# Queries and values of the sparse attention split at their projections, the last gates tied to the memory branch, gate stores issued by ACT

## The chip, the cores and the metric

The kernel runs on one core of a Trainium2 chip. Five engines work side by side, each with its own queue of instructions that it takes in order: PE (TensorE, matrix products and transposes), DVE (VectorE), ACT (ScalarE), POOL (GpSimd) and SP (SyncE, which only issues DMA transfers here). The metric is the time of one execution on the device, in microseconds (us); lower is better.

## The reference

One inference step of a hybrid streaming encoder on 1024 prompt tokens and 64 sample tokens (1088 together, width 1024). What matters here:

```python
qa = rope(rmsnorm(qa.reshape(B, T, N_HEADS_A, HD_A), g_qa), pos)      # 8 heads of 64
ka = rope(rmsnorm(ka.reshape(B, T, N_KV_A, HD_A), g_ka), pos)         # 2 heads of 64
va = va.reshape(B, T, N_KV_A, HD_A)
...
logits = jnp.einsum('bthgd,btjhd->bthgj', q, k_sel, ...) * (HD_A ** -0.5)   # selected keys only
probs = jax.nn.softmax(logits, axis=-1).astype(va.dtype)
out = jnp.einsum('bthgj,btjhd->bthgd', probs, v_sel)
...
# memory branch: 4 heads of 128 against 256 memory tokens
logits = jnp.einsum('bthd,bmhd->bhtm', qm, mk, ...) * (HD_M ** -0.5)
return jnp.einsum('bhtm,bmhd->bthd', probs, mv).reshape(B, T, D_MEM_ATT)
...
ga, gb, gm = jnp.split(jax.nn.sigmoid(gates...), N_BRANCH, axis=-1)
mixed = ga * (a @ w_oa) + gb * (b @ w_ob) + gm * (m @ w_om)
```

After that come an output projection and a SwiGLU feed-forward, which the change does not touch.

## The kernel before

Precise products are made from split numbers: a float is kept as a rounded high part and a remainder (names with `hi`/`h` and `lo`/`l`), and one product becomes three matmuls, hi x hi, hi x lo and lo x hi. ACT or POOL makes the high part, DVE subtracts to get the low one. Tokens are worked on in nine blocks (eight of 128, one of 64).

The stages around the change, with their places in the profiled execution (us from the span's start):

- Queries of the memory branch are projected (326 to 397; `qn` stored to `q_m` in DRAM).
- Queries of the sparse attention, `w_qa`, in two halves of nine blocks (397 to 460). Each block is 24 matmuls from token blocks and a weight `tmhi`/`tmlo`, held in one buffer; then come four squares on ACT (`hjunk`), a power on POOL (`hr`), the scaling on DVE (`qn`), the rotation on DVE (`rope`, `qr`), and a store to `q_a` in DRAM. The selection of keys runs beside this on DVE and ACT.
- Keys and values, `w_kv` (460 to 530). A block's keys go through the same chain with two heads, then are split (`kd`: a cast on ACT, a subtraction on DVE), transposed four times on PE, copied by ACT (`kt`) and stored to `k_t`; values go to `v_a`.
- The memory branch (530 to 655), in steps `t` of two halves: queries are loaded (`qn<-q_m`), transposed and split (`qh`, `ql`); logits `lg`; softmax `ex`; probabilities are transposed and multiplied with the values.
- Attention (684 to 870), with blocks in the order 2, 0, 1, 3, 8, 4, 5, 6, 7. `queries_t` loads a block's queries, splits them (`qs`: cast on ACT, subtraction on DVE), transposes the eight heads on PE and copies the result on ACT into `qT`. Ahead of it all values are loaded (`vf`) and split into `vb` in ten pieces.

The order on each engine is fixed when the program is built, by a scheduler with priorities. Three groups of products have low priority and are scheduled where PE has nothing else (`fl` in PSUM, three banks): the gates (`fill_gate`; 96 products of 24 matmuls with `hh`, `hl`, a tanh on ACT into `fsg` and a store), the w_ob products (`fill_ob`, which load a gate as `fpt`), and the w_om products (`fill_om`, which load `gt`). The last 24 gates (72 to 95) go to `side_a`; before, the call for them stands behind the memory branch. SP issues all their stores, as nearly all other transfers. `raw`, `fraw` are loads of weights; a lane is one of eight semaphores that transfers take in turn, and an instruction that uses a transfer's result, or its lane again, waits for it.

Of the kernel before, what the change touches and what calls it, by code (L numbers as in the profile page):

```python
# [22 lines left out]
NB = 9  # L23
# [22 lines left out]
def encoder_step(ctx: ExitStack, tc: tile.TileContext, a: dict, o: list):  # L46
# [30 lines left out]
    def mm(dt=F32):  # L77
        return psum[0].tile([128, 512], dt, name="mm", tag="mm", bufs=n_mm[0])
# [22 lines left out]
    def wblock(src, shape, raw=None, hl_=None):  # L101
# [10 lines left out]
        lo_of(lo, raw, hi)  # L112
        return hi.rearrange(pat, **kw), lo.rearrange(pat, **kw)

    def matmul3(ps, pairs):
        n = len(pairs) * 3
        i = 0
        for lh, ll, rh, rl in pairs:
            for l, r in ((lh, rh), (lh, rl), (ll, rh)):
                PE.matmul(ps, l, r, start=i == 0, stop=i == n - 1)  # L120
                i += 1

    def rstd(r, ss, inv):
# [60 lines left out]
    side_m = dram.tile([KT, 2, 128, T], F32, name="side_m")  # L184
    side_a = dram.tile([KT, 2, 128, T], F32, name="side_a")
    gate_b = dram.tile([KT, 128, T], F32, name="gate_b")
    q_a = dram.tile([T, 512], F32, name="q_a")
    q_m = dram.tile([T, 512], F32, name="q_m")
    k_t = dram.tile([128, 2, 2, SEQ + PAST + DEC], F32, name="k_t")
    v_a = dram.tile([T, 128], F32, name="v_a")  # L190
    mem_k = dram.tile([256, 512], F32, name="mem_k")
    mem_v = dram.tile([256, 512], F32, name="mem_v")

# [3 lines left out]
    def raw_tile():  # L197
        return wp.tile([128, 1024], F32, name="raw", tag="raw", bufs=3)
# [274 lines left out]
    with tc.tile_pool(name="qa", bufs=1) as qp:  # L473
        cosa = qp.tile([128, NB, HDA], F32, name="cosa")
        sina = qp.tile([128, NB, HDA], F32, name="sina")

        def tables(gname, scale=None):
            SP.dma_start(cosa, a["cos_a"].rearrange("(b p) d -> p b d", p=128))
            SP.dma_start(sina, a["sin_a"].rearrange("(b p) d -> p b d", p=128))
            g1 = qp.tile([128, HDA], F32, name="g1", tag="g1", bufs=2)  # L480
            g2 = qp.tile([128, HDA], F32, name="g2", tag="g2", bufs=2)
            bcast_row(g1, a[gname], 0, HDA)
            bcast_row(g2[:, :32], a[gname], 32, 32)
            bcast_row(g2[:, 32:], a[gname], 0, 32)
            if scale:
                for g_ in (g1, g2):
                    G.tensor_scalar(g_, g_, scale, 1.0, op0=OP.mult, op1=OP.mult)
            G.tensor_tensor(cosa, cosa, g1[:, None, :].to_broadcast([128, NB, HDA]), op=OP.mult)
            G.tensor_tensor(sina, sina, g2[:, None, :].to_broadcast([128, NB, HDA]), op=OP.mult)

        tables("g_qa", -HDA ** -0.5)
        for half in range(2):
            w = tm_weights(qp, a["w_qa"][half], 256)
            for b in range(NB):
                t0, n = TS[b]
                ps = token_major(w, b, 256)
                qn = qp.tile([128, 4, HDA], F32, name="qn", tag="qn", bufs=2)
                head_norm(qp, ps, n, 4, HDA, qn[:n])
                qr = qp.tile([128, 4, HDA], F32, name="qr", tag="qr", bufs=2)
                rope(qp, qr[:n], qn[:n], n, 4, HDA, cosa[:, b], sina[:, b])  # L500
                SP.dma_start(q_a[t0:t0 + n, half * 256:(half + 1) * 256], qr[:n].rearrange("p h d -> p (h d)"))

        def key_split(src, n):
            kd = qp.tile([128, 2, 2, 2, HDA], F32R, name="kd", tag="kd", bufs=2)
            bc = src[:, :, None, :].to_broadcast([n, 2, 2, HDA])
            A.copy(kd[:n, :, 0], bc)
            V.tensor_tensor(kd[:n, :, 1], bc, kd[:n, :, 0].bitcast(F32), op=OP.subtract)
            return kd

        def keys_t(kd, n, c0):  # L510
            ps = mm(F32R)
            for j in range(4):
                PE.transpose(ps[:, j * 128:j * 128 + n],
                             kd[:n, j // 2, j % 2].rearrange("p s d -> p (s d)"), ident_r[:n, :n])
            kt = qp.tile([128, 2, 2, 128], F32R, name="kt", tag="kt", bufs=2)
            A.copy(kt[:, :, :, :n].rearrange("p k s t -> p (k s) t"), ps.rearrange("p (j t) -> p j t", j=4)[:, :, :n])
            SP.dma_start(k_t[:, :, :, c0:c0 + n], kt[:, :, :, :n].bitcast(F32))

        kc = raw_tile()[:, :128]
        SP.dma_start(kc, a["cache_a_k"])  # L520
        last = (key_split(kc.rearrange("p (k d) -> p k d", k=2), 128), 128, SEQ)
        tables("g_ka")
        w = tm_weights(qp, a["w_kv"], 256)
        for b in range(NB):
            t0, n = TS[b]
            ps = token_major(w, b, 256)
            kn = qp.tile([128, 4, HDA], F32, name="qn", tag="qn", bufs=2)[:, :2]
            head_norm(qp, ps[:, :128], n, 2, HDA, kn[:n])
            kr = qp.tile([128, 4, HDA], F32, name="qr", tag="qr", bufs=2)
            rope(qp, kr[:n, :2], kn[:n], n, 2, HDA, cosa[:, b], sina[:, b])  # L530
            A.copy(kr[:n, 2:].rearrange("p h d -> p (h d)"), ps[:, 128:])
            kf = kr[:n, :2].rearrange("p h d -> p (h d)")
            vf = kr[:n, 2:].rearrange("p h d -> p (h d)")
            SP.dma_start(o[2][t0:t0 + n] if b < 8 else o[8], kf)
            SP.dma_start(o[3][t0:t0 + n] if b < 8 else o[9], vf)
            SP.dma_start(v_a[t0:t0 + n], vf)
            kd = key_split(kr[:n, :2], n)
            if last:
                keys_t(*last)
            last = (kd, n, t0 if b < 8 else SEQ + PAST)  # L540
        keys_t(*last)
# [39 lines left out]

    for c0, cn in CH:
        for f, w in enumerate(first):
            SP.dma_start(gate_b[f, :, c0:c0 + cn], fsig(w, c0, cn))
    fill_gate(8, gate_b, 2, 8)
    fill_gate(16, side_m[:, 0], 0, 8)
    fill_ob()
# [2 lines left out]
    if True:  # L592
# [3 lines left out]
        with tc.tile_pool(name="matw", bufs=1) as mp:  # L596
# [33 lines left out]
            def queries(t0, n, half):  # L630
# [3 lines left out]
                for h in range(2):  # L634
                    PE.transpose(ps[:, h * n:(h + 1) * n], qn[:, h * 128:(h + 1) * 128], ident[:n, :n])
                return ps[:, :2 * n]

            for half in range(2):
                hs2 = slice(2 * half, 2 * half + 2)
# [80 lines left out]
                for t in range(11):  # L720
# [4 lines left out]
                    if 0 <= t - 3 < 8:  # L725
                        values_of(t - 3, exs[t - 3], pp_)
                    sample(t)


    rest = [(f, ci) for ci in range(3) for f in range(KT)]  # L730
    fill_gate(0, side_a[:, 0], 0, 8)
    for _ in range(1):
        fill_om(*rest.pop(0))
    kv_c = tc.tile_pool(name="kvp", bufs=1)
# [116 lines left out]

    aoh, aol = bh, bl
    ORDER = (0, 2, 1, 3)
    KEYS_AT = {0: (384, 768), 3: (768, SEQ + PAST + DEC)}
    with tc.tile_pool(name="att", bufs=1, side="right") as ap_:

        def wide(name):
            return ap_.tile([128, 1024], F32, name=name, tag="pr", bufs=11)

        vf = [wide("vf").rearrange("p (b c) -> p b c", c=128) for _ in range(2)]  # L860
        SP.dma_start(vf[0], v_a[:SEQ].rearrange("(b p) c -> p b c", p=128))
        SP.dma_start(vf[1][:, 0], a["cache_a_v"])
        SP.dma_start(vf[1][:64, 1], v_a[SEQ:])
        for b0, b1, n in ((0, 3, 128), (3, 6, 128), (6, 8, 128), (8, 9, 128), (9, 10, 64)):
            for kv in range(2):
                vs = vf[b0 // 8][:n, b0 % 8:b0 % 8 + b1 - b0, kv * HDA:(kv + 1) * HDA]
                A.copy(vb[:n, b0:b1, kv, 0], vs)
                lo_of(vb[:n, b0:b1, kv, 1], vs, vb[:n, b0:b1, kv, 0])

        def queries_t(b):  # L870
            t0, n = TS[b]
            q = ap_.tile([128, HA, HDA], F32, name="q", tag="q", bufs=2)
            ld = SP.dma_start(q[:n].rearrange("p h d -> p (h d)"), q_a[t0:t0 + n])
            if b in KEYS_AT:
                with tc.issue_after(ld.ins):
                    load_keys(*KEYS_AT[b])
            qs = ap_.tile([128, HA, 2, HDA], F32R, name="qs", tag="qs", bufs=1)
            A.copy(qs[:n, :, 0], q[:n])
# [588 lines left out]
```

## Time and profile before

| | |
|---|---|
| Median of 3 runs | 1745.0 us (1744.95 to 1747.08) |
| The profiled execution | 1742.28 us |
| Its span, first to last instruction | 1740.5 us |
| Mean granted clock of TensorE | 0.997 of full speed |
| PE, DVE, ACT, POOL busy | 97%, 68%, 46%, 24% of the span |

Busy shares are means over stages with different limits, so a stage has to be read by its own windows. A wait is put down to the engine whose semaphore came last. The span is what the trace shows; 1.8 us of the execution lie around it.

### The profile page before, as it was taken

Reading aid. Unit: us, or ns where it says so; the run is one execution under the profiler, and the core shown is the slowest. Engines: PE = TensorE matmul, PEld = TensorE weight load, DVE = VectorE, ACT = ScalarE, POOL = GpSimd, SP = SyncE. Lnnn points to the kernel's source line nnn. Section 1 sums busy time; section 2 is a strip of 40 time slices with the busy share of each in tenths; the row PEclk is TensorE's granted clock in tenths of the full one; section 3 lists DMA queues with packets and bytes.
Section 4 is the critical chain, followed back from the end, with each engine's and each line's share of the span. In section 5 each row is a group of like instructions: output and inputs, shape, how many; then the busy total and the mean of one; then the engine's idle time right before and its main releaser. Section 6 shows DMA issues by size and latency. Waiting matters only on the chain.

```text
span 1740.5 us, 32481 instructions
## 1 busy us (share of the span) xinstructions
PE 1687.7 (97%) x12074; PEld 1637.3 (94%) x12074; DVE 1181.5 (68%) x2597; ACT 809.0 (46%) x1949; POOL 409.6 (24%) x444
## 2 busy tenths in 40 slices
PE   7999999999999999899899999999999999999999
PEld 6999999999999999787698998999999999999999
DVE  6566999999964442788874687666658556465553
ACT  5457667746633441569722343334334333353431
POOL 4110423345511212775303442000101000000000
PEclk9999999999999999999999999999999999999999
DMA  7212541223367324760273326443545443497661
GB/s 233 65 62 67 173 138 47 71 84 109 95 183 223 106 93 144 260 196 2 87 259 114 118 82 220 167 142 106 191 145 179 148 153 121 136 349 256 207 195 53
DMA packets 154829, 251.38 MB, mean 144 GB/s; under 512 B 25127, under 2 KB 101279, under 8 KB 154670
## 3 DMA queue, kind: packets, MB, share of 16 engines
q1 hardware_dynamic: 154670, 249.30, 44.0%
q8 instruction: 95, 1.56, 0.4%
q14 instruction: 64, 0.52, 0.1%
HBM read 174.15 MB, written 75.09 MB: 143 GB/s over the span
## 4 chain that ended last, share of the span: by engine, by line
PE 59%; DVE 6%; DMA 4%; issue 2%; POOL 2%; ACT 2%; SPq 0%; DVEq 0%; ACTq 0%; POOLq 0%
PE mm L1129 24%; PE mm L1352 12%; PE mm L120 10%; PE fl L120 8%; PE acc L933 1%; PE tr L903 1%; DVE lo L86 1%; PE mm L926 1%; DVE wlo L86 1%; DVE fr L1083 1%; DMA u<-tg 1%; DMA side_a<-gt 1%; DMA gt<-side_m 0%; DVE ws L1090 0%; PE mm L615 0%
## 5 line engine op out<-in xcount | busy, mean ns | idle before, releaser
L1129 PE MATMUL mm<-hi,whi 128*128 128x288 f32 (+1 forms) x1120 | 323.0, 289 | 2.3 <-ACT whi L1121 2.3
L1129 PE MATMUL mm<-lo,whi 128*128 128x288 f32 (+1 forms) x1120 | 323.4, 289 | 0.0
L1129 PE MATMUL mm<-hi,wlo 128*128 128x288 f32 (+1 forms) x1120 | 323.4, 290 | 0.0
L1129 PEld LDWEIGHTS mm<-hi,whi 128*128 128x128 f32 x1120 | 211.8, 189 | 3.0 <-ACT whi L1121 3.0
L1129 PEld LDWEIGHTS mm<-lo,whi 128*128 128x128 f32 x1120 | 211.8, 189 | 0.0
L1129 PEld LDWEIGHTS mm<-hi,wlo 128*128 128x128 f32 x1120 | 211.0, 189 | 0.2 <-DVE wlo L86 0.2
L120 PE MATMUL fl<-hh,whi 128*128 128x362 f32 (+1 forms) x576 | 190.1, 331 | 0.4 <-ACT hh L133 0.4
L120 PE MATMUL fl<-hl,whi 128*128 128x362 f32 (+1 forms) x576 | 190.2, 330 | 0.0
L120 PE MATMUL fl<-hh,wlo 128*128 128x362 f32 (+1 forms) x576 | 189.8, 330 | 0.0
L1352 PE MATMUL mm<-uh,wh 128*128 128x256 f32 (+1 forms) x600 | 171.4, 289 | 0.9 <-ACT wh L1342 0.9
L1352 PE MATMUL mm<-ul,wh 128*128 128x256 f32 (+1 forms) x600 | 171.7, 288 | 0.0
L1352 PE MATMUL mm<-uh,wl 128*128 128x256 f32 (+1 forms) x600 | 170.4, 288 | 0.0
L120 PE MATMUL mm<-tmlo,hh 128*128 128x256 f32 (+3 forms) x432 | 123.0, 287 | 1.1 <-DVE tmlo L86 1.0
L120 PE MATMUL mm<-tmhi,hh 128*128 128x256 f32 (+3 forms) x432 | 121.8, 287 | 2.0 <-POOL tmhi L96 2.0
L120 PE MATMUL mm<-tmhi,hl 128*128 128x256 f32 (+3 forms) x432 | 122.5, 286 | 0.0
L86 DVE TENSOR_TENSOR wlo<-raw,whi 128x1024 fp32r<-128x1024 f32 (+1 forms) x75 | 75.2, 1014 | 65.2 <-ACT whi L1121 38.9
L777 ACT ACTIVATE junk_a<-score,cand_a,sgn_a 128x512 f16<-128x512 f32 (+2 forms) x93 | 95.5, 1027 | 41.9 <-DVE cand_a L794 21.8
L1352 PEld LDWEIGHTS mm<-uh,wh 128*128 128x128 f32 x600 | 112.4, 188 | 1.3 <-ACT wh L1342 1.3
L1352 PEld LDWEIGHTS mm<-ul,wh 128*128 128x128 f32 x600 | 112.7, 188 | 0.0
L1352 PEld LDWEIGHTS mm<-uh,wl 128*128 128x128 f32 x600 | 112.2, 188 | 0.1
L120 PEld LDWEIGHTS fl<-hh,whi 128*128 128x128 f32 x576 | 108.6, 189 | 1.4 <-issue 0.8
L120 PEld LDWEIGHTS fl<-hl,whi 128*128 128x128 f32 x576 | 108.5, 188 | 0.6
(395 smaller groups left out, 4563.0 us busy)
## 6 DMA issues: line engine op xcount, KB each, us to landing
uf<-u SPq DMA_DIRECT2D x75, 272.0 KB, 4.3
raw<-in_w_up_dram SPq DMA_DIRECT2D x26, 512.0 KB, 4.3
fraw<-in_w_gates_dram SPq DMA_DIRECT2D x24, 512.0 KB, 3.6
fr<-in_w_gate_dram SPq DMA_DIRECT2D x22, 512.0 KB, 4.2
dr<-in_w_down_dram SPq DMA_DIRECT2D x22, 512.0 KB, 5.7
s<-dr SPq DMA_DIRECT2D x22, 512.0 KB, 3.1
raw<-s SPq DMA_DIRECT2D x44, 256.0 KB, 3.8
side<-side_a SPq DMA_DIRECT2D x8, 1088.0 KB, 6.9
```

The costliest lines, as they stand in the source:

```text
L86: V.tensor_tensor(lo, src, hi.bitcast(F32), op=OP.subtract)
L120: PE.matmul(ps, l, r, start=i == 0, stop=i == n - 1)
L777: A.activation(junk[:n, :nk], sc, AF.Sign, bias=bj, scale=1.0 if scale is None else scale[:n, j:j + 1], accum_out=sj)
L903: PE.matmul(lg[:n, i * 512:i * 512 + cn], qT[:, h, :n], kT[:, kv, s, k0 + c:k0 + c + cn], start=s == 0, stop=s == 1)
L926: PE.transpose(pt[:cn, i * n:(i + 1) * n], probs[i][:, c:c + cn], ident[:n, :n])
L933: PE.matmul(acc, vv, r, start=ji == 0 and i == 0, stop=ji == nj - 1 and i == 1)
L1083: V.scalar_tensor_tensor(hb[e][:, :n], ys[i][:, kk], gffn_c[:, kk:kk + 1], rb[:, :n], op0=OP.mult, op1=OP.mult)
L1129: PE.matmul(dst[i], l, r, start=start and j == 0, stop=stop and j == 11, skip_group_check=True)
L1352: PE.matmul(acc[f, i], l[:, fs], r[:, cs], start=start and j == 0, stop=stop and j == 2, skip_group_check=True)
```

## The change

Queries are split and transposed where they are projected, and kept in DRAM transposed (`q_t`); attention loads `qT` with one transfer. Values are split where they are projected (`v_t`), and attention loads `vb` in two to three transfers, tied behind loads of queries. The last 24 gates are issued from inside the memory branch's steps, each tied behind a matmul of an earlier step. All gate stores are issued by ACT in place of SP. The tile pool `pr` of attention has 12 buffers for 11.

```diff
-    q_a = dram.tile([T, 512], F32, name="q_a")
+    q_t = dram.tile([NB, 128, HA, 128], F32, name="q_t")
-    v_a = dram.tile([T, 128], F32, name="v_a")
+    v_t = dram.tile([SEQ + PAST + DEC, 2, 2, HDA], F32, name="v_t")
...
+        def split(name, src, n, heads):
+            s = qp.tile([128, heads, 2, HDA], F32R, name=name, tag=name, bufs=2)
+            A.copy(s[:n, :, 0], src)
+            V.tensor_tensor(s[:n, :, 1], src, s[:n, :, 0].bitcast(F32), op=OP.subtract)
+            return s
+
+        def four_t(s, n, dst):
+            ps = mm(F32R)
+            for j in range(4):
+                PE.transpose(ps[:, j * 128:j * 128 + n], s[:n, j], ident_r[:n, :n])
+            t = qp.tile([128, 4, 128], F32R, name="kt", tag="kt", bufs=2)
+            A.copy(t[:, :, :n], ps.rearrange("p (j t) -> p j t", j=4)[:, :, :n])
+            SP.dma_start(dst, t[:, :, :n].bitcast(F32))
...
-                SP.dma_start(q_a[t0:t0 + n, half * 256:(half + 1) * 256], qr[:n].rearrange("p h d -> p (h d)"))
+                if last:
+                    four_t(*last)
+                qs = split("kd", qr[:n], n, 4).rearrange("p h s d -> p h (s d)")
+                last = (qs, n, q_t[b, :, half * 4:half * 4 + 4, :n])
+        four_t(*last)
...
+        def keep_v(src, n, r0):
+            vd = split("vd", src, n, 2)
+            SP.dma_start(v_t[r0:r0 + n], vd[:n].bitcast(F32))
...
-            SP.dma_start(v_a[t0:t0 + n], vf)
             kd = key_split(kr[:n, :2], n)
-            if last:
-                keys_t(*last)
-            last = (kd, n, t0 if b < 8 else SEQ + PAST)
-        keys_t(*last)
+            four_t(*last)
+            c0 = t0 if b < 8 else SEQ + PAST
+            keep_v(kr[:n, 2:], n, c0)
+            last = (kd, n, keys_to(c0, n))
+        four_t(*last)
...
             for c0, cn in CH:
-                SP.dma_start(dst[f, :, c0:c0 + cn], fsig(w, c0, cn))
+                A.dma_start(dst[f, :, c0:c0 + cn], fsig(w, c0, cn))
...
+            steps = []
+            gates = [(f, c) for f in range(KT) for c in CH]
+            gate_w = []
+
+            def gates_between(lag=2):
+                while gates and (not lag or (KT * 3 - len(gates)) * 11 // 12 <= len(steps) - 1):
+                    f, (c0, cn) = gates.pop(0)
+                    if c0 == 0:
+                        gate_w[:] = fgate(f)
+                    with tc.issue_after(steps[max(0, len(steps) - 1 - lag)]):
+                        A.dma_start(side_a[f, 0, :, c0:c0 + cn], fsig(gate_w, c0, cn))
...
                     sample(t)
+                    steps.append(last_mm[0])
+                    gates_between()
...
-    fill_gate(0, side_a[:, 0], 0, 8)
+    gates_between(0)
...
-        vf = [wide("vf").rearrange("p (b c) -> p b c", c=128) for _ in range(2)]
...
-                A.copy(vb[:n, b0:b1, kv, 0], vs)
-                lo_of(vb[:n, b0:b1, kv, 1], vs, vb[:n, b0:b1, kv, 0])
+        def load_values(b0, b1):
+            SP.dma_start(vb[:, b0:b1].rearrange("p b k s d -> p b (k s d)").bitcast(F32),
+                         v_t[b0 * 128:b1 * 128].rearrange("(b p) k s d -> p b (k s d)", p=128))
...
-            q = ap_.tile([128, HA, HDA], F32, name="q", tag="q", bufs=2)
-            ld = SP.dma_start(q[:n].rearrange("p h d -> p (h d)"), q_a[t0:t0 + n])
...
-            qs = ap_.tile([128, HA, 2, HDA], F32R, name="qs", tag="qs", bufs=1)
-            A.copy(qs[:n, :, 0], q[:n])
-            V.tensor_tensor(qs[:n, :, 1], q[:n], qs[:n, :, 0].bitcast(F32), op=OP.subtract)
-            ps = tr(F32R)
-            for h in range(HA):
-                PE.transpose(ps[:, h * 128:h * 128 + n], qs[:n, h].rearrange("p s d -> p (s d)"), ident_r[:n, :n])
-            qT = ap_.tile([128, HA, 128], F32R, name="qT", tag="qT", bufs=2)
-            A.copy(qT[:, :, :n], ps.rearrange("p (h t) -> p h t", h=HA)[:, :, :n])
+            qT = ap_.tile([128, HA, 128], F32R, name="qT", tag="qT", bufs=3)
+            ld = SP.dma_start(qT[:, :, :n].bitcast(F32), q_t[b, :, :, :n])
```

The order on PE where the last query block ends and the first key block begins, before (`mm<-tmhi` and `mm<-tmlo` are a block's products, `64x256` the last, short block, `kd` the transposes of the cached keys):

```order
L120 MATMUL mm<-tmhi,hl 64x256
L120 MATMUL fl<-hh,whi 128x362
L120 MATMUL fl<-hl,whi 128x362
L120 MATMUL fl<-hh,wlo 128x362
...
L120 MATMUL mm<-tmhi,hh 128x256 [waits DVE_49,Pool_49]
L513 MATMUL mm<-ident_r,kd 128x128 [waits DVE_49]
L513 MATMUL mm<-ident_r,kd 128x128 x3
```

The same place in the change (here `kd` are the split queries of the last two blocks):

```order
L122 MATMUL mm<-tmhi,hl 64x256
L503 MATMUL mm<-ident_r,kd 128x128 [waits DVE_49,PE_49]
L503 MATMUL mm<-ident_r,kd 128x128 x3
L503 MATMUL mm<-ident_r,kd 128x64 [waits DVE_49]
L503 MATMUL mm<-ident_r,kd 128x64 x3
L122 MATMUL mm<-tmhi,hh 128x256 [waits Pool_49]
```

A gate's 24 `fl` products stood between the last query product and the first key product; now the transposes of the last two query blocks stand there, and no `fl`.

The order on PE at the end of the keys, before (the last key block's transposes, `128x64`, and what follows):

```order
L513 MATMUL mm<-ident_r,kd 128x64 [waits PE_49,Activation_49]
L120 MATMUL fl<-bh,wlo 128x362
L120 MATMUL fl<-bh,whi 128x362
L120 MATMUL fl<-bl,whi 128x362
L120 MATMUL fl<-bh,wlo 128x362
L513 MATMUL mm<-ident_r,kd 128x64 [waits DVE_49]
L513 MATMUL mm<-ident_r,kd 128x64 x2
L120 MATMUL fl<-bh,whi 128x362
L120 MATMUL fl<-bl,whi 128x362
```

The same place in the change, on to the memory branch's first logits (`raw` memory keys, `qn` its queries, `kh`, `qh` the logits):

```order
L503 MATMUL mm<-ident_r,kd 128x64 [waits PE_49,Activation_49]
L650 MATMUL mm<-ident,raw 128x128 [waits DMAHW4_49,PE_49]
L650 MATMUL mm<-ident,raw 128x128 x3
L503 MATMUL mm<-ident_r,kd 128x64 [waits DVE_49]
L503 MATMUL mm<-ident_r,kd 128x64 x2
L658 MATMUL mm<-ident,qn 128x128 [waits DMAHW3_49,DMAHW4_49,DMAHW2_49,DMAHW5_49,DMAHW1_49,DMAHW6_49,DMAHW0_49,DMAHW7_49,Activation_49,Pool_49]
L658 MATMUL mm<-ident,qn 128x128
L658 MATMUL mm<-ident,qn 128x128 [waits DMAHW1_49]
L658 MATMUL mm<-ident,qn 128x128
L122 MATMUL mm<-kh,qh 128x256 [waits Activation_49]
L122 MATMUL mm<-kl,qh 128x256 [waits DVE_49]
```

The w_ob products (`fl<-bh`, `fl<-bl`) that stood around the last key transposes have moved into the first half of the queries, and nothing of low priority stands between the seventh query block and the first logits.

The order on SP at the same place, in the change (the load of the memory branch's queries behind the stores of keys and values):

```order
L506 DMA k_t<-kt 512x1x128 [waits DMAHW2_49,Activation_49]
L558 DMA out_dram<-qr 64x128 [waits DMAHW3_49,Activation_49]
L557 DMA out_dram<-qr 64x128 [waits DMAHW4_49,DVE_49]
L537 DMA v_t<-vd 64x256 [waits DMAHW5_49,DVE_49]
L646 DMA raw<-in_cache_mem_v_dram 128x2x256 [waits DMAHW6_49,PE_49]
L506 DMA k_t<-kt 512x1x64 [waits DMAHW7_49,Activation_49]
L655 DMA qn<-q_m 128x256 [waits DMAHW2_49,DMAHW3_49,DMAHW1_49,DMAHW4_49,DMAHW0_49,DMAHW5_49,DVE_49,DMAHW7_49,PE_49,Pool_49]
```

The load waits for all eight lanes, that of the last `k_t` store among them; before, it waited for two lanes and PE.

## Rows read from the trace of the kernel before

**Rows 1.** The page: engines, busy us, share, instructions.

```profile
PE 1687.7 (97%) x12074; PEld 1637.3 (94%) x12074; DVE 1181.5 (68%) x2597; ACT 809.0 (46%) x1949; POOL 409.6 (24%) x444
```

**Rows 2.** Windows: us, then busy time by engine, PEclk, DMA share, GB/s.

```profile
326.00:330.00 4.00, 3.79 (x16) 3.31 (x17) 4.00 (x6) 3.29 (x7) 1.14 (x2) 0.59 0.45 156
397.00:460.00 63.00, 61.94 (x495) 61.44 (x494) 61.66 (x193) 46.35 (x200) 34.22 (x44) 1.00 0.25 81
460.00:530.00 70.00, 66.39 (x474) 64.88 (x473) 48.62 (x143) 20.78 (x74) 18.94 (x25) 1.00 0.66 189
530.00:655.00 125.00, 123.52 (x834) 120.38 (x833) 53.69 (x113) 48.96 (x139) 27.05 (x43) 1.00 0.41 131
684.00:870.00 186.00, 168.19 (x1014) 142.21 (x1015) 153.09 (x330) 128.52 (x303) 109.86 (x125) 1.00 0.45 145
684.00:710.00 26.00, 20.84 (x121) 18.56 (x122) 16.39 (x41) 11.54 (x33) 15.54 (x16) 1.00 0.94 321
780.00:840.00 60.00, 57.14 (x337) 46.28 (x337) 54.32 (x113) 54.32 (x115) 29.01 (x34) 1.00 0.01 2
```

**Rows 3.** Groups by shape, 684 to 870: busy, mean ns, idle before.

```profile
L884 ACT CAST qT<-tr 128x1024 fp32r<-128x1024 f32 x8 | 8.1, 1011 | 7.0 <-PE tr L882 7.0
L879 DVE TENSOR_TENSOR qs<-q,qs 128x512 fp32r<-128x512 f32 x8 | 6.4, 796 | 2.4 <-ACT qs L878 1.3 <-PE fl L120 0.7
L878 ACT CAST qs<-q 128x512 fp32r<-128x512 f32 x8 | 5.0, 624 | 0.0
```

**Rows 4.** Timeline at attention's start: start us, us, engine, instruction, idle before.

```profile
688.76 2.10 ACT L867 CAST vb<-vf 128x192 fp32r<-128x192 f32 x10 [6.60 <-DMA vf<-v_a]
...
694.35 0.86 PE L882 MATMUL tr<-ident_r,qs 128*128 128x128 f32 x8 [1.09 <-DVE qs L879]
```

**Rows 5.** PE's waits, 684 to 870: us in total, times, longest.

```profile
PE tr L903 <- DVE mx L907: 3.9, 8, 1.0
```

**Rows 6.** Timeline of one key block, 500 to 506.

```profile
500.83 0.28 PE L120 MATMUL mm<-tmhi,hl 128*128 128x256 f32 x1
...
504.23 0.41 ACT L506 CAST kd<-qr 128x256 fp32r<-128x256 f32 x1 [0.66 <-DVE qr L153]
...
504.67 0.42 DVE L507 TENSOR_TENSOR kd<-qr,kd 128x256 fp32r<-128x256 f32 x1 [0.47 <-ACT kd L506]
```

**Rows 7.** The tile kt: durations ns min/median/max, and its transfers.

```profile
L516 ACT CAST kt<-mm x10: 372/586/588, 460.6 to 522.7; 128x512 fp32r<-128x512 f32 x9, 128x256 fp32r<-128x256 f32 x1
...
DMA to landing us min/median/max: 2.6/3.0/4.2
```

**Rows 8.** The chain that ended last: 24 products of a block.

```profile
479.91 2.94 PE mm L120 x24
```

**Rows 9.** Groups by shape, 397 to 460, a query block's chain.

```profile
L125 POOL TENSOR_TENSOR hr<-hr,mhalf 128x4 f32<-128x4 f32 x16 | 18.0, 1124 | 1.3
...
L208 DVE TENSOR_TENSOR qn<-mm,hr 128x256 f32<-128x256 f32 x16 | 6.6, 415 | 1.2 <-POOL hr L125 1.2
```

**Rows 10.** Timeline from the last query products to the first key product.

```profile
455.43 0.28 PE L120 MATMUL mm<-tmhi,hl 128*64 128x256 f32 x1
...
456.73 2.67 POOL L96 TENSOR_SCALAR tmhi<-raw 128x1024 fp32r<-128x1024 f32 x2
...
460.03 0.28 PE L120 MATMUL mm<-tmhi,hh 128*128 128x256 f32 x1
```

**Rows 11.** The tensor q_m: its transfers, stores and loads.

```profile
DMA to landing us min/median/max: 1.7/2.1/5.3
```

**Rows 12.** Timeline of the memory branch's first queries.

```profile
539.11 0.87 DVE L654 SCALAR_TENSOR_TENSOR ql<-mm,gqm_c,qh 128x256 fp32r<-128x256 f32 x2
```

**Rows 13.** PE's waits, 300 to 546: us in total, times, longest.

```profile
PE fl L120 <- DVE fpt L561: 4.6, 3, 2.0
PE mm L120 <- POOL tmhi L96: 2.0, 1, 2.0
```

**Rows 14.** SP's waits over the span: us in total, times, longest.

```profile
SPq L549 <- ACT fsg L235: 144.0, 43, 5.6
```

More of the change, by code (lines that the diff above doesn't have):

```diff
@@ L113, in wblock @@
         return hi.rearrange(pat, **kw), lo.rearrange(pat, **kw)
+    last_mm = [None]
     def matmul3(ps, pairs):
@@ L119, in matmul3 @@
             for l, r in ((lh, rh), (lh, rl), (ll, rh)):
-                PE.matmul(ps, l, r, start=i == 0, stop=i == n - 1)
+                last_mm[0] = PE.matmul(ps, l, r, start=i == 0, stop=i == n - 1).ins
                 i += 1
@@ L489, in tables @@
             G.tensor_tensor(sina, sina, g2[:, None, :].to_broadcast([128, NB, HDA]), op=OP.mult)
+        def split(name, src, n, heads):
[10 more added lines that the diff above has]
+            SP.dma_start(dst, t[:, :, :n].bitcast(F32))
         tables("g_qa", -HDA ** -0.5)
+        last = None
         for half in range(2):
@@ L507, in key_split, with keys_to @@
             V.tensor_tensor(kd[:n, :, 1], bc, kd[:n, :, 0].bitcast(F32), op=OP.subtract)
[L508 to L517, printed above, removed]
+            return kd.rearrange("p k s c d -> p (k s) (c d)")
+        def keys_to(c0, n):
+            return k_t[:, :, :, c0:c0 + n].rearrange("p k s t -> p (k s) t")
+        def keep_v(src, n, r0):
+            vd = split("vd", src, n, 2)
+            SP.dma_start(v_t[r0:r0 + n], vd[:n].bitcast(F32))
+        vc = raw_tile()[:, :128]
+        SP.dma_start(vc, a["cache_a_v"])
+        keep_v(vc.rearrange("p (k d) -> p k d", k=2), 128, SEQ)
         kc = raw_tile()[:, :128]
         SP.dma_start(kc, a["cache_a_k"])
-        last = (key_split(kc.rearrange("p (k d) -> p k d", k=2), 128), 128, SEQ)
+        last = (key_split(kc.rearrange("p (k d) -> p k d", k=2), 128), 128, keys_to(SEQ, 128))
         tables("g_ka")
@@ L585, in encoder_step @@
         for f, w in enumerate(first):
-            SP.dma_start(gate_b[f, :, c0:c0 + cn], fsig(w, c0, cn))
+            A.dma_start(gate_b[f, :, c0:c0 + cn], fsig(w, c0, cn))
     fill_gate(8, gate_b, 2, 8)
@@ L853, in encoder_step @@
     ORDER = (0, 2, 1, 3)
+    BLOCKS = (2, 0, 1, 3, 8, 4, 5, 6, 7)
     KEYS_AT = {0: (384, 768), 3: (768, SEQ + PAST + DEC)}
@@ L857, in wide @@
         def wide(name):
-            return ap_.tile([128, 1024], F32, name=name, tag="pr", bufs=11)
-        vf = [wide("vf").rearrange("p (b c) -> p b c", c=128) for _ in range(2)]
[L861 to L866, printed above, removed]
-                A.copy(vb[:n, b0:b1, kv, 0], vs)
-                lo_of(vb[:n, b0:b1, kv, 1], vs, vb[:n, b0:b1, kv, 0])
@@ L870, in queries_t @@
-        def queries_t(b):
-            t0, n = TS[b]
-            q = ap_.tile([128, HA, HDA], F32, name="q", tag="q", bufs=2)
-            ld = SP.dma_start(q[:n].rearrange("p h d -> p (h d)"), q_a[t0:t0 + n])
-            if b in KEYS_AT:
-                with tc.issue_after(ld.ins):
-                    load_keys(*KEYS_AT[b])
-            qs = ap_.tile([128, HA, 2, HDA], F32R, name="qs", tag="qs", bufs=1)
-            A.copy(qs[:n, :, 0], q[:n])
-            V.tensor_tensor(qs[:n, :, 1], q[:n], qs[:n, :, 0].bitcast(F32), op=OP.subtract)
-            ps = tr(F32R)
-            for h in range(HA):
-                PE.transpose(ps[:, h * 128:h * 128 + n], qs[:n, h].rearrange("p s d -> p (s d)"), ident_r[:n, :n])
-            qT = ap_.tile([128, HA, 128], F32R, name="qT", tag="qT", bufs=2)
-            A.copy(qT[:, :, :n], ps.rearrange("p (h t) -> p h t", h=HA)[:, :, :n])
+            return ap_.tile([128, 1024], F32, name=name, tag="pr", bufs=12)
@@ new lines, in load_values @@
+        def load_values(b0, b1):
+            SP.dma_start(vb[:, b0:b1].rearrange("p b k s d -> p b (k s d)").bitcast(F32),
+                         v_t[b0 * 128:b1 * 128].rearrange("(b p) k s d -> p b (k s d)", p=128))
+        def queries_t(b):
+            n = TS[b][1]
+            qT = ap_.tile([128, HA, 128], F32R, name="qT", tag="qT", bufs=3)
+            ld = SP.dma_start(qT[:, :, :n].bitcast(F32), q_t[b, :, :, :n])
+            with tc.issue_after(ld.ins):
+                if b == BLOCKS[0]:
+                    load_values(0, 4)
+                if b == 3:
+                    load_values(4, 9)
+                    SP.dma_start(vb[:64, 9].rearrange("p k s d -> p (k s d)").bitcast(F32),
+                                 v_t[SEQ + PAST:].rearrange("p k s d -> p (k s d)"))
+                if b in KEYS_AT:
+                    load_keys(*KEYS_AT[b])
@@ L951, in fill @@
                 n -= 1
-        for b in (2,0,1,3,8,4,5,6,7):
+        for b in BLOCKS:
             qT = queries_t(b)
```

## The prediction

> **What bounds it now.** The page's engine rows come first: PE is busy 97% of the 1740.5 us span [rows 1], so a change can gain only where PE idles or runs at half clock, and loses wherever it uncovers a wait. PE's own work stays: the same matmuls, and 72 query transposes that move. So I looked at the stages by windows [rows 2]. While queries are projected (397 to 460 us) DVE is the full engine, 61.66 of 63 us, and PE idles only 1.1. While keys and values are projected (460 to 530) PE idles 3.6. Attention (684 to 870) is 186 us long with PE busy 168.19, so 17.8 us of recorded idle: 5.2 of it at the start (684 to 710), the rest later, where from 780 to 840 DVE and ACT are each busy 54.32 of 60 us. The kernel before hides its long chains under low-priority products, the gates and w_ob products that are scheduled into PE's holes (`fl`). So there are two questions: what does attention get back, and are there products left to cover the chains in the projections?
>
> **What attention gets back.** Out of it go, by the means of [rows 3], nine `qs` casts (5.6 us) and nine `qT` copies (9.1) on ACT, with ten `vb` casts that ran as one piece of 2.1 [rows 4]: 16.8 us. On DVE go nine `qs` subtractions (7.2) and ten for `vb`, some 3. On PE, 72 transposes at 0.86 us for eight [rows 4]: 7.7 us. At the start ACT idled 6.6 us until `vf` had landed [rows 4], then came the `vb` casts and the chain of cast, subtraction, transposes and copy; the first transposes start at 694.35, ten us into the stage. One load into `qT` should close this start: 5 us. Later the largest named PE wait is on DVE's `mx`, 3.9 us in 8 [rows 5], on an engine that loses 10 of its 153 busy us. The idle that goes lies between 5 us (the start alone) and 17.8 (all of it). I take 13, nearer the upper end, since both engines that were 90% full are relieved.
>
> **What the projections take on.** The same splits come back in smaller pieces, 18 for queries and 10 for values. By the key block's rows a cast is 0.41 us and a subtraction 0.42 [rows 6], and a copy of four transposes 0.59 [rows 7]: some 20 us of ACT, 10 of DVE. In 397 to 460 DVE has no room for its 7.6 (18 x 0.42), but PE has more fill meanwhile: in the changed order the w_ob products and gates 72 to 75 stand in the first query half. I put the slower DVE at 2 us (0 if fill covers it, 4 if half of it shows).
>
> What comes after costs more. The ties let gates 76 and on start only with the memory branch, and the w_ob products are used up in the query stage. From the seventh query block to the first `lg` the order has no `fl` at all, and five chains stand bare:
>
> (a) The last query blocks. A block's transposes stand right after the next block's 24 products: 2.94 us [rows 8] and 0.43 for their own four transposes, 3.4 us of work. A key block's chain, from the end of its last product (500.83 + 0.28) to that of its `kd` subtraction (504.67 + 0.42), is 4.0 us [rows 6]. A query block has two squares more on ACT (taken at 0.4, as the cast), an `hr` power of 1.12 us [rows 9] for some 0.7, and five DVE passes over twice the width (`qn` 0.415 [rows 9]; 0.1 each): I take 5.7. As each waits for the block before it, two blocks take 5.7 + 3.4, or 4.55 a block for 3.4 of work: 1.15 lost on each of three, 3.4.
>
> (b) The switch to keys. The ninth block's transposes stand straight behind its products. In its chain POOL first does two `tmhi` (2.67 us for both [rows 10]) and DVE two `tmlo`, which puts `hr` and `qn` off by some 1.3: 5.7 + 1.3, less 0.4 of the other block's transposes, 6.6 us of hole. Before, the gap between the last query product at 455.43 and the first key product at 460.03 [rows 10] held one gate's 24 products.
>
> (c) Key blocks. The first transpose needs only the `kd` cast, which ends 3.5 us after the products [rows 6], against 3.4 of work: little, but more where ACT does squares of the next block first. 2 us for all nine (1 to 5).
>
> (d) The last key block's remaining transposes wait for its whole chain of 4.0, with 0.4 of others before them: 3.6 us.
>
> (e) The memory branch's first query. Its load goes into space that the projections leave, so it stands on SP behind every lane, the last `k_t` store too: `kt` copy 0.4 and 3.0 from issue to landing (2.6 to 4.2) [rows 7], then 2.1 for the load (1.7 to 5.3) [rows 11], transposes 0.4, `qh` and `ql` 0.44 each [rows 12]: 6.8, less 0.8 for the mem-key transposes: 6 us (4.5 to 10). Before, w_ob products filled this.
>
> Together 3.4 + 6.6 + 2 + 3.6 + 6 = 21.6 (11 if the chains are a quarter shorter and catch up with each other, 27 at the upper ends). Where one hole lets the next chain catch up: minus 3. Of the 4.6 us of waits on `fpt` before [rows 13], some 2 go.
>
> **The clock.** After the 2.0 us wait for `tmhi` [rows 13] PE's granted clock was 0.59 from 326 to 330 us [rows 2]: most of that at 1.2 GHz in place of 2.4, worth (1 - 0.59) x 4 = 1.6 us of work. (b) and (e) are longer holes: 2.5 for both (0 to 3.3), as part of the slow stretch falls into waits. The Trainium skill (TensorE: Matmul & The Clock Gate, HAM oscillation) says that a PE that keeps idling between bursts of matmuls is throttled and pays the way up again after each; that row shows one such fall. By it every hole could cost this, a rival below.
>
> One more gate stands ahead of the first memory-query product, where PE waited for `tmhi`: minus 2 (0 to 3.6).
>
> **The rest.** Tying the gates gives PE nothing in the memory branch: it is full there, 123.52 of 125 us [rows 2]; a tail of plain gates is only spread over the steps. As for stores on ACT, SP stood 144.0 us on `fsg`, 43 times [rows 14], but none of PE's larger waits [rows 5, 13] is on what SP then issued late. So SP's relief is worth nothing, or 1 us. The 72 issues sit on an engine with room (ACT is busy 46% [rows 1]), but a store can wait for a DMA lane and ACT's next work with it. No row shows such an issue; between -1 and 8 us I take 1.
>
> **Sum**, against the profiled execution (1742.3, the span and 1.8 around it): 21.6 - 3 - 2 + 2.5 + 2 - 2 - 13 + 1 = + 7.1, so 1749.4. The median of the runs is 2.7 above that execution: **1752 us**. About 0.2%, 3.5 us, can be told from no change in this kernel.
>
> **Rivals**, as medians.
> - Attention decides (faster). Its length is set by DVE and ACT, not by PE: then all 17.8 us go, and the 7.7 of transposes too, which elsewhere lie in the holes. That is 25 us against 20.1 for all the rest: 1740. For it: DVE and ACT at 90% from 780 to 840. Against: the chains through `mx` keep their length. It decides from 20 us of shorter attention on. Chance 0.25.
> - The same time. POOL starts `tmhi` before the query products end, so (b) is half as long, and the store in (e) lands early: 8 us less, 1744. Against: `tmhi` has one buffer, read by those very products. 0.18.
> - Stores on ACT hold it up: 24 in the memory branch with 0.4 us of lane wait ahead of `ex` and `qh`, 9 us more: 1761. Against: ACT has over half its time free there. 0.10.
> - The clock falls at each hole, five more at 1.6: 1760. Against: 460 to 530, with waits of up to 2.0 us, ran at 1.00 [rows 2, 13]. 0.05.
> - The change doesn't do what it says: the query chains were prefetched and hidden, so only the start's 5 us come back, 1760. For it: after the start no `qs` or `qT` is among the larger waits. 0.06.
> - The forecast, 1748.5 to 1757: 0.36.
>
> So slower has 0.36 + 0.10 + 0.05 + 0.06 = 0.57, same 0.18, faster 0.25. The range, 1738 to 1764, leaves out the faster half of the first rival and the upper ends of the slower ones, each about 0.1.
>
> **What would show it.** In the changed trace: over 15 us of PE idle between the seventh query block and the first `lg`, its waits on `kd` and `qn`; one or two stretches of half clock there; an attention stage some 18 to 21 us shorter, its transposes included, without the wait for `vf`; a memory branch as full as before. I am wrong if PE's waits on `kd` sum to under 5 us (the chains are shorter than I read them), if attention shrinks by over 25 us, or if ACT idles on store lanes.

## The result, and the profile after

The change is slower: 1765.4 us (median, 1763.4 to 1767.8) against 1745.0, a ratio of 1.0109 with a 95% interval of 1.0089 to 1.0128. That is just above the predicted range (1738 to 1764), and about three times the predicted 7 us. The profiled execution took 1765.88 us, its span 1764.1, against 1742.28. One run of all, of e_untied below, had a granted clock of 0.751 and took 2048.6 us; it is left out of the times and ratios.

The page of the changed kernel, engine rows and the granted clock in 40 slices (tenths of full speed):

```profile
PE 1694.8 (96%) x12074; PEld 1645.5 (93%) x12074; DVE 1180.6 (67%) x2606; ACT 816.6 (46%) x1967; POOL 398.8 (23%) x444
...
PEclk9999999999998899899999999999999999999999
```

DVE and ACT are as busy as before [rows 1]: the work has moved, not gone. PE does the same 12074 matmuls and is 7.1 us longer busy, at a mean granted clock of 0.986 for 0.997; outside its busy time it idles 69.3 us of the span for 52.8. These two, 7.1 and 16.5, make up the 23.6 us between the two executions. Windows of the changed kernel (us, busy time of PE, PEld, DVE, ACT and POOL, PEclk, DMA share, GB/s), cut at the starts of the first and last products of its stages; the last two are attention and its start, cut as in [rows 2], counted from the end of the last gate:

```profile
402.00:536.00 134.00, 127.69 (x916) 125.89 (x914) 99.00 (x293) 66.37 (x236) 33.82 (x47) 1.00 0.48 148
536.00:545.00 9.00, 1.47 (x11) 1.16 (x10) 6.01 (x10) 2.54 (x13) 5.09 (x4) 0.64 0.45 126
545.00:580.00 35.00, 31.56 (x250) 30.55 (x251) 14.28 (x56) 15.95 (x65) 10.20 (x18) 0.95 0.45 128
580.00:592.00 12.00, 3.43 (x16) 2.20 (x16) 3.15 (x10) 4.21 (x14) 0.87 (x2) 0.62 0.54 153
592.00:713.00 121.00, 121.00 (x801) 118.31 (x802) 48.46 (x103) 49.58 (x139) 23.20 (x43) 0.98 0.32 100
715.40:895.30 179.90, 165.84 (x951) 141.85 (x950) 147.49 (x312) 116.26 (x276) 106.26 (x125) 0.96 0.52 170
715.40:741.40 26.00, 22.84 (x109) 19.84 (x108) 14.63 (x37) 9.39 (x30) 15.79 (x22) 0.80 0.99 350
```

Read down the second number, PE's busy time. The query stage (402 to 536; it now holds all w_ob products and four of the last 24 gates; the gates are 72 products by the trace, not 96) idles 6.3 us, where it idled 1.1 [rows 2]. The switch from queries to keys (536 to 545) is all but empty: 7.5 idle of 9. The key blocks idle 3.4. From the last key product to the first `lg` (580 to 592) 8.6 of 12 are idle. The memory branch with its tied gates is full. Attention is 179.9 us long where it was 186: 6.1 shorter, with 14.1 us idle for 17.8 [rows 2].

PE's waits from 397 to 620 us (us in total, times, longest):

```profile
PE mm L503 <- DVE kd L497: 10.2, 4, 7.0
PE mm L503 <- ACT kd L528: 6.5, 5, 3.1
PE mm L658 <- DMA qn<-q_m: 5.4, 1, 5.4
PE fl L122 <- ACT fsg L237: 2.0, 1, 2.0
PE fl L122 <- DVE fpt L584: 1.6, 1, 1.6
```

The first three are the chains that the prediction named, (a) and (b), (c) and (d), and (e): 22.1 us. Before, none of them stood among the larger waits [rows 13]. The one of 7.0 us, in the timeline (start, us, engine, instruction, idle before):

```profile
536.22 2.17 POOL L96 TENSOR_SCALAR tmhi<-raw 128x1024 fp32r<-128x1024 f32 x2 [2.42 <-PE mm L122]
...
537.42 3.18 DVE L86 TENSOR_TENSOR tmlo<-raw,tmhi 128x1024 fp32r<-128x1024 f32 x2 [0.94 <-POOL tmhi L96]
...
539.60 1.88 POOL L127 TENSOR_TENSOR hr<-hr,mhalf 64x4 f32<-64x4 f32 x1
...
543.70 0.42 DVE L497 TENSOR_TENSOR kd<-qr,kd 64x256 fp32r<-64x256 f32 x1 [0.47 <-ACT kd L496]
...
544.17 0.69 PE L503 MATMUL mm<-ident_r,kd 64*128 64x64 f32 x4 [7.03 <-DVE kd L497]
```

POOL splits the key weights first, then takes the last query block's power, then DVE and ACT finish; PE's transposes are the next thing in its queue all that time.

### The profile page after: what moved, and what is told of

Read it like the earlier page. It is cut to its first block, busy times and chain, and to the rows that moved or that the text cites. A ratio compares the mean times of both kernels' runs of the same rounds, so it can differ in the third digit from the quotient of the medians.

```text
span 1764.1 us, 32488 instructions
## 1 busy us (share of the span) xinstructions
PE 1694.8 (96%) x12074; PEld 1645.5 (93%) x12074; DVE 1180.6 (67%) x2606; ACT 816.6 (46%) x1967; POOL 398.8 (23%) x444
## 4 chain that ended last, share of the span: by engine, by line
PE 79%; DVE 9%; ACT 4%; issue 3%; POOL 2%; DMA 2%; SPq 0%; ACTq 0%; DVEq 0%; POOLq 0%
PE mm L1160 24%; PE mm L122 19%; PE fl L122 17%; PE mm L1383 12%; PE tr L934 1%; PE acc L964 1%; DVE junk_v L818 1%; ACT junk_a L815 1%; DVE wlo L86 1%; DVE lo L86 1%; PE mm L335 1%; PE mm L957 1%; DMA raw<-s 1%; DVE fr L1114 1%; PE mm L503 1%
```

## The experiments

Each was compared with runs of the kernel before on the same chip; ratios are to it. The windows are of one trace each.

**The change without its ties (e_untied)**

```diff
                     sample(t)
-                    steps.append(last_mm[0])
-                    gates_between()
...
-    gates_between(0)
+    fill_gate(0, side_a[:, 0], 0, 8)
```

> The change without its ties: the last 24 gates are free again, so they can stand in the holes of the query and key projections. Theory (bare chains, and the clock falling behind them): the stretch from the first query product to the first lg gets back 20 us or more (less 4 us a gate that moves into it), no half clock there; but the gates are then used up before the second half of the memory branch, where PE waits in their place. Together 1745 to 1757 us. Rival (the extra work of DVE and ACT in the projections is what costs): the holes stay as waits at other places and the time stays at 1762 or more.

1754.2 us (1750.3 to 1757.1; the trace is of the fastest run), ratio 1.0063 (1.0036 to 1.0090). Windows: the switch, the end of keys to the first `lg`, and the second half of the memory branch up to the first attention products.

```profile
538.30:550.20 11.90, 11.90 (x76) 11.64 (x74) 7.57 (x10) 3.75 (x14) 6.96 (x5) 1.00 0.54 171
595.70:615.50 19.80, 19.80 (x125) 19.22 (x124) 5.13 (x12) 6.98 (x18) 1.93 (x3) 1.00 0.59 178
657.60:711.70 54.10, 41.39 (x262) 36.76 (x261) 31.50 (x67) 26.56 (x77) 16.84 (x28) 0.91 0.50 163
```

Both holes are full, at full clock, and the fill is then missing later: 12.7 us of idle from 658 on, where the gates have run out. As the theory had it, there is one stock of fill, and the ties choose which chains go bare. The choice has a price: without the ties the change is 11 us faster by the medians and 8 by the ratios, about half of its loss.

**Queries alone (e_q_only) and values alone (e_v_only)**, each in the kernel before, with free gates and stores on SP.

```diff
# e_q_only: values as before, queries as in the change
-                SP.dma_start(q_a[t0:t0 + n, half * 256:(half + 1) * 256], qr[:n].rearrange("p h d -> p (h d)"))
+                if last:
+                    four_t(*last)
+                qs = split("kd", qr[:n], n, 4).rearrange("p h s d -> p h (s d)")
+                last = (qs, n, q_t[b, :, half * 4:half * 4 + 4, :n])
...
# e_v_only: queries as before, values as in the change
-            SP.dma_start(v_a[t0:t0 + n], vf)
...
+            keep_v(kr[:n, 2:], n, c0)
...
```

> The kernel before with the queries' part alone (untied gates, stores on SP, values as before). Theory (fill runs short): gates cover the query and key projections, but the second half of the memory branch is left without fill, 10 to 20 us of waits there, against 4 us from attention: 1748 to 1758. Rival (the queries' part is good by itself, the ties spoil it): 1742 or less.

> The kernel before with the values' part alone. Theory: it closes part of attention's start and costs next to nothing in the key projections, whose chain is hidden: 1740 to 1745. Rival (the added work for values delays the key projections): 1748 or more.

Queries alone: 1757.1, ratio 1.0064 (1.0040 to 1.0088). Its memory branch has the same bare second half (the window from its last gate to the first attention products):

```profile
663.00:718.00 55.00, 41.01 (x252) 36.63 (x251) 31.88 (x73) 26.79 (x82) 14.90 (x26) 0.88 0.47 155
```

Values alone: 1741.2, ratio 0.9975 (0.9965 to 0.9984), faster than both kernels. The start of attention, from the last gate to the first keys-times-queries product, idles 0.8 us in its trace, against 2.9 in the kernel before (second line) and 0.7 in the change (third):

```profile
681.60:693.90 12.30, 11.54 (x71) 11.22 (x71) 5.87 (x8) 2.63 (x4) 7.83 (x7) 1.00 0.70 238
681.30:696.30 15.00, 12.06 (x70) 11.04 (x68) 9.40 (x19) 4.15 (x14) 7.93 (x7) 1.00 0.75 246
712.70:723.50 10.80, 10.06 (x62) 9.77 (x61) 5.42 (x6) 1.06 (x2) 4.45 (x5) 1.00 0.69 231
```

**All but the queries (e_no_q)**: values, ties and stores on ACT.

```diff
-                if last:
-                    four_t(*last)
-                qs = split("kd", qr[:n], n, 4).rearrange("p h s d -> p h (s d)")
-                last = (qs, n, q_t[b, :, half * 4:half * 4 + 4, :n])
+                SP.dma_start(q_a[t0:t0 + n, half * 256:(half + 1) * 256], ...)
```

> The whole change but the queries' part: values split at the projection, gates tied, all gate stores on ACT, queries as before. Theory (the queries' part uses up the fill and gives attention next to nothing): 1740 to 1747, no long wait of PE between the queries and the first lg. Rival (ties or ACT stores carry a good part of the loss): 1752 or more.

1743.3, ratio 0.9989 (0.9975 to 1.0003). Taking the queries' part out takes the whole loss out. From its last query products to the first `lg`, at 551:

```profile
464.00:551.00 87.00, 85.98 (x596) 84.28 (x594) 56.64 (x158) 25.19 (x93) 23.55 (x30) 1.00 0.71 207
```

**Ties alone (e_tied_only), stores on ACT alone (e_act_only), the change with stores on SP (e_sp)**

```diff
# e_tied_only, in the kernel before
+                    steps.append(last_mm[0])
+                    gates_between()
# e_act_only, in the kernel before
-                SP.dma_start(dst[f, :, c0:c0 + cn], fsig(w, c0, cn))
+                A.dma_start(dst[f, :, c0:c0 + cn], fsig(w, c0, cn))
# e_sp, in the change: the same lines, the other way
```

> The kernel before with the ties alone. Theory: the ties cost only because queries' and values' splits use up the other fill; here the w_ob products still cover the key projections, so 1742 to 1750. Rival (ties cost by themselves): 1755 or more.

> The kernel before with its gate stores issued by ACT, nothing else. Theory (the issuer is worth little, a stall of ACT on a lane now and then): 1744 to 1750. Rival (ACT stores alone cost the 5 us by which the change with SP stores was faster): 1750 or more.

> The change with all gate stores on SP. Theory: the store's issuer is worth at most 2 us, 1763 to 1767. Rival (ACT held up by stores and their lanes): 5 us or more back, 1760 or less.

Ties alone: 1744.9, ratio 1.0005 (0.9989 to 1.0021). ACT stores alone: 1745.6, 1.0002 (0.9990 to 1.0015). The change with SP stores: 1759.7, 1.0089 (1.0062 to 1.0117). So neither ties nor ACT stores cost anything in the kernel before. The change itself is 5.7 us faster by the medians with SP stores, which is what the rival expected, and 3.5 by the ratios. But the two intervals overlap, and the order of the fill differs too: up to some 5 us of the loss may belong to the issuer, and these runs don't settle it.

**The work put back beside (e_load), and a little work put on the chain (e_chain)**

```diff
# e_load, per block: into a tile that nobody reads; the pool pr has 11 buffers again
+            A.copy(again[:, :4, :n], src[:, :4])
+            V.tensor_tensor(again[:, 4:, :n], src[:, :4], again[:, :4, :n].bitcast(F32), op=OP.subtract)
+            A.copy(again[:, :, :n], src)
# e_chain, per softmax
+                    V.tensor_scalar(my, mx, 1.0, None, op0=OP.mult)
-                    A.activation(pr, pr, AF.Exp, bias=mx, ...)
+                    A.activation(pr, pr, AF.Exp, bias=my, ...)
```

> The change with the removed ACT and DVE work put back into attention as work that nobody waits for: for each block a 0.6 us cast and a 1.0 us copy on ACT and a 0.7 us subtraction on DVE, into a tile that is not read. Theory A (attention is set by the chain from PE over DVE's mx, ACT's exp and POOL to PE; the removed work had lain beside it): attention from the first keys-times-queries product to the first w_oa product stays within 3 us of the change's 171 us. Theory B (the relief of DVE and ACT did pay its 8 to 10 us, and something else took them back): attention gets 8 us or more longer, 1772 or more in all.

> The change with one more short DVE instruction in each of attention's 72 softmax chains: the maximum is multiplied by one into a second tile, which exp reads in place of it; some 0.15 us each, about as much DVE time in all (7 to 11 us) as the subtractions that the change took out and a little more. Theory (the length of the chain from PE over DVE and ACT back to PE sets attention, not the engines' sums): attention from the first keys-times-queries product to the first w_oa product gets 5 to 15 us longer, while the larger load off the chain (24 us of ACT and DVE) cost 1.5. Rival (such work is hidden on the chain too, since other blocks' products fill PE): 3 us or less.

e_load: 1766.9, ratio 1.0128 (1.0108 to 1.0147). Attention from its first keys-times-queries product to its last, and on to the first w_oa product:

```profile
722.00:868.40 146.40, 136.97 (x783) 116.34 (x782) 127.27 (x278) 108.62 (x256) 98.68 (x115) 0.97 0.51 169
868.40:894.80 26.40, 21.21 (x124) 16.18 (x123) 20.67 (x38) 18.14 (x37) 8.41 (x8) 1.00 0.36 133
```

The same two windows in the kernel before, and then in the change:

```profile
696.30:843.20 146.90, 136.90 (x834) 116.63 (x834) 124.30 (x275) 106.43 (x255) 94.83 (x113) 1.00 0.42 135
843.20:869.60 26.40, 21.21 (x125) 16.20 (x123) 20.67 (x38) 18.17 (x37) 8.15 (x8) 1.00 0.37 135
723.50:865.80 142.30, 134.66 (x775) 115.87 (x774) 121.51 (x268) 96.28 (x236) 97.44 (x117) 0.96 0.53 173
865.80:894.90 29.10, 23.42 (x134) 18.51 (x132) 21.67 (x39) 19.26 (x40) 5.44 (x5) 0.94 0.33 121
```

The two windows together last 173.3 us before, 171.4 in the change and 172.8 in e_load, and PE idles 15.2, 13.3 and 14.6 us in them. What the change removed from ACT and DVE here costs 1.4 us when it is back. e_chain: 1773.5, ratio 1.0146 (1.0128 to 1.0163); the same two windows, and the added instruction:

```profile
726.30:873.40 147.10, 137.98 (x774) 116.03 (x774) 129.65 (x337) 93.85 (x234) 98.75 (x117) 0.97 0.53 168
873.40:902.80 29.40, 22.36 (x134) 17.27 (x132) 21.89 (x42) 20.63 (x42) 5.43 (x5) 1.00 0.33 120
```

```profile
L941 DVE TENSOR_SCALAR my<-mx x72: 131/145/156, 730.0 to 876.0; 128x1 f32<-128x1 f32 x64, 64x1 f32<-64x1 f32 x8
```

They last 176.5 us: 72 x 0.145 = 10.4 us on the chain cost 5.1, half of them, at the lower end of what was expected. The w_om products also stand in other places in e_chain, so this speaks for the chain but does not prove it. That the removed work had been nearly free is shown by e_load.

**The holes filled with useless matmuls (e_warm)**: 38, 18 and 30, which write a bank that nobody reads.

```diff
+        keep_busy(38)
         four_t(*last)
...
+        keep_busy(18)
         four_t(*last)
+        keep_busy(30)
```

> The change with 86 matmuls without use (into a spare bank) that fill the three large holes: 38 at the switch from queries to keys, 18 before the last key transposes, 30 behind them. The chains stay as long as they are. Theory (half of the loss there is the clock, which falls behind the holes): no half clock from 530 to 600 us, 9 to 13 us faster than the change, 1752 to 1757. Rival (the holes cost their idle time alone): 1763 to 1770, the useless products hidden or a little over.

1767.7 (1765.8 to 1773.2; the trace is of the slowest run), ratio 1.0142 (1.0113 to 1.0171): no gain. The switch, the end of keys to the first `lg`, and attention's two windows as above:

```profile
538.80:547.50 8.70, 7.28 (x49) 7.01 (x47) 5.59 (x9) 2.42 (x11) 4.99 (x4) 1.00 0.40 117
582.00:597.90 15.90, 10.83 (x66) 9.71 (x65) 3.57 (x11) 4.53 (x13) 0.88 (x2) 0.95 0.43 120
730.60:872.30 141.70, 133.34 (x773) 112.79 (x774) 123.56 (x268) 96.10 (x236) 99.17 (x117) 1.00 0.54 174
872.30:901.60 29.30, 23.49 (x134) 18.51 (x132) 21.87 (x39) 19.17 (x40) 5.45 (x5) 0.94 0.32 120
```

PE was kept at full clock through the switch, and the switch lasted 8.7 us against 9.0: its length is that of the chain. The stretch to `lg` got longer (15.9 against some 12), since the key transposes now stood behind the useless products. The price of the clock this run leaves open, for the theory's condition was not met: the slow stretches moved beside the holes.

```profile
530.00:540.00 10.00, 7.98 (x56) 7.80 (x55) 4.21 (x12) 3.26 (x17) 3.02 (x4) 0.83 0.14 52
550.00:560.00 10.00, 8.90 (x69) 8.69 (x68) 3.54 (x14) 3.81 (x16) 3.65 (x6) 0.90 0.27 77
600.00:610.00 10.00, 10.00 (x55) 9.78 (x55) 2.35 (x7) 3.44 (x12) 1.72 (x4) 0.84 0.43 133
```

Attention, the two windows together, lasted 171.0 us at 1.00 and 0.94, against 171.4 at 0.96 and 0.94 in the change.

**Gates placed by hand (e_place2)**: four free, two tied behind the last query product, three behind the last key transposes, fifteen over the steps.

```diff
+            for tie in (qa_free, qa_free, qa_free, qa_free, qa_end, qa_end, kv_end, kv_end, kv_end):
+                gate(tie)
```

> The change with its last gates placed by hand: four free, two tied behind the last query product, three behind the last key transposes, fifteen over the memory branch's steps. Theory (the holes at the switch and before the first lg are what the change loses, 8 and 10 us): both close, with no half clock in them; 14 to 20 us faster than the change, 1746 to 1752, less up to 5 us if the memory branch now lacks fill. Rival (the chains move the wait elsewhere): 1760 or more.

1755.2, ratio 1.0057 (1.0038 to 1.0076): 10 us back, not 14 to 20. Windows: the switch, the stretch to `lg`, and from the last gate to the first attention products.

```profile
535.70:544.70 9.00, 9.00 (x59) 8.71 (x57) 6.02 (x10) 3.40 (x14) 5.51 (x5) 1.00 0.36 108
579.70:599.40 19.70, 19.70 (x124) 19.01 (x124) 5.59 (x13) 6.92 (x18) 1.92 (x3) 1.00 0.59 174
694.20:712.90 18.70, 15.75 (x84) 15.03 (x83) 7.39 (x9) 2.62 (x5) 5.70 (x7) 0.82 0.82 284
```

Both holes are closed without an idle us. Part of that is lost again at attention's start, now 18.7 us from the last gate with some 3 idle and a granted clock of 0.82.

**More fill at attention's start (e_v_om)**: the values' part alone, with three w_om products pulled forward.

```diff
-        for i in range(3):
+        for i in range(6):
             fill_om(*rest.pop(0), other=i % 3 > 0)
```

> The values' part alone, with three more w_om products put at attention's start. Theory (attention starts with short products and waits, behind which the clock falls; more fill there holds it up): 1736 to 1741, no half clock at attention's start. Rival (the fill is then missing later in attention): 1742 or more.

1745.2, ratio 1.0002 (0.9988 to 1.0016): the gain of the values' part is gone, as the rival expected. That the fill was missing later is not shown: the trace, of the fastest run, took 1741.6 us, as long as that of e_v_only.

## Why the prediction went wrong

**The bare chains: right.** The prediction put (a) to (e) at 21.6 us; PE's waits on them are 22.1. (b) was 6.6 and measured 7.0; (d) 3.6 and 3.1; (e) 6 and 5.4; (a) 3.4 and 3.2 (10.2 less 7.0); (c) 2 and 3.4 (6.5 less 3.1). They are bare because the fill has gone elsewhere: e_untied and e_place2 close (b) and (e) with gates. The 3 us taken off because chains would overlap did not come.

**What attention gets back: the step that failed.** "I take 13, nearer the upper end, since both engines that were 90% full are relieved." Measured, attention's idle fell from 17.8 us to 14.1: 3.7. A little over half of that is the start (2.9 us idle before, 0.7 in the change), which e_v_only closes with the values alone. The rest hardly responded to the relief: DVE and ACT lost 6 and 12 us between the same cuts, and in e_load the work stood there again for 1.4 us. The fifth rival, "the query chains were prefetched and hidden, so only the start's 5 us come back", was the case; it had a chance of 0.06. The evidence against the 13 stood in the rows: no wait on `qs` or `qT` among PE's larger ones [rows 5] after the start. A busy share of 90% was read as a bound; by e_load it was mostly work beside the chain. PE's waits on the chains of attention, in the change (723 to 895) and before (696 to 870):

```profile
PE acc L964 <- DVE ot L969: 4.9, 6, 1.9
PE tr L934 <- DVE mx L938: 4.4, 7, 1.0
PE tr L903 <- DVE mx L907: 3.9, 8, 1.0
PE acc L933 <- DVE ot L938: 2.8, 4, 1.3
```

They have not become shorter.

**The clock: a second term, put too small.** 2.5 us were predicted for stretches at half clock; PE's busy time grew by 7.1 for the same matmuls. The long stretches:

```profile
538.00:549.00 11.00, 4.83 (x24) 4.76 (x25) 5.01 (x9) 1.14 (x4) 6.09 (x5) 0.53 0.63 161
582.00:597.00 15.00, 8.09 (x33) 7.00 (x34) 4.81 (x14) 5.00 (x13) 0.18 (x1) 0.54 0.70 211
729.00:740.00 11.00, 9.64 (x34) 7.78 (x35) 5.66 (x23) 6.57 (x23) 8.32 (x12) 0.53 1.06 386
```

The first two lie around the two large holes; the third follows waits of under 1 us on `mx`. It was not every hole, as the fourth rival had it: the key blocks from 550 to 580 idled 3.4 us at 1.00, as here in a third of them:

```profile
560.00:570.00 10.00, 8.48 (x72) 8.07 (x71) 4.92 (x20) 5.50 (x24) 2.49 (x6) 1.00 0.42 124
```

What these stretches cost depends on whether PE is needed there. In the switch it hardly is: at 1.00 it was 8.7 us long for 9.0. In the memory branch PE was busy 121.00 of 121.00 us at a mean of 0.98, which is worth some 2 us of work (an estimate, 0.02 x 121). For attention the traces disagree. e_warm, at 1.00 from the first keys-times-queries product to the last, was 0.4 us shorter than the change up to the first w_oa product. e_untied was at 1.00 too, with as many matmuls and as much idle:

```profile
711.70:851.10 139.40, 131.93 (x774) 112.31 (x774) 122.42 (x268) 95.21 (x236) 102.08 (x117) 1.00 0.50 158
```

That is 2.9 us shorter than the 142.3 of the change. So what the clock costs in attention stays open. The Trainium skill (TensorE: Matmul & The Clock Gate, HAM oscillation) puts the cost of a throttled stretch at half of its time. By that the three stretches would cost some 17 us (an estimate from the page's half and the granted clocks above); the trace has 7.1 us more of busy time, as PE worked in only 22.6 of the 37.

**The transposes.** They were counted as moved at no cost, and in PE's total that holds: 12074 matmuls in both kernels. In attention 7.7 us went, but PE's busy time there fell by only 2.4 (168.19 to 165.84). The rest is the slower clock and more w_om products in that stage; the two were not separated. This is why attention is 6.1 us shorter, in place of 18 to 21.

**The rest.** The slower DVE in the query stage, put at 2 us, does not show by itself. The stage's idle of 6.3 us is made up of (a) and of two waits of fill, 2.0 on `fsg` and 1.6 on `fpt`; that the idle without (a) grew by about 2 is luck. The wait for `tmhi` ahead of the memory queries, put at minus 2, is still there:

```profile
PE mm L122 <- POOL tmhi L96: 2.4, 1, 2.4
```

The gate ahead of it moved the wait and left it as long (2.0 before [rows 13]). Ties and the ACT issuer alone are worth nothing in the kernel before.

**The sum again.** The prediction adds up to 4.6 us more idle on PE and 2.5 for the clock, 7.1. Measured are 16.5 us more idle and 7.1 more busy time, 23.6 in the profiled executions. Of the 11.9 us of idle that were missed, 9.3 are attention's, 3.5 the overlap of the chains that did not come, and 2.4 `tmhi`; smaller terms went some 3 us the other way. The forecast of "slower" came true because the chains were read rightly.

## What to carry to other kernels

Fill is a stock: before moving work into a stage, count the low-priority products that cover its chains and say which chain goes bare when they are used up there. Ties decide which one, and here the choice was about half of the loss. A busy share, even of 90%, does not say that removing work shortens a stage; look for the removed instruction among what the bounding engine waits for, and if it isn't there, put the work back beside the chain as a test. A part of a change that is good by itself (here the values, 0.25% faster alone) can be hidden in a bundle that loses, so time the parts.

## What the hardware showed that was not expected

TensorE's granted clock stayed low for longer around the two large holes, 0.53 over 11 us and 0.54 over 15 us, where one wait of 2.0 us in the kernel before left 0.59 over 4 us [rows 2]. Filling the holes with useless matmuls did not keep it up: in e_warm it was 1.00 through the switch, where PE was busy 7.28 of 8.70 us, and fell beside it, to 0.83 from 530 to 540 and 0.84 from 600 to 610. In the last of these PE was busy all the time.
